# Value tiles ahead of the receptance tiles, and the recurrence queued one tile later with denser steps

## The chip, the cores and the metric

One Trainium2 chip, one of its cores. The metric is device time in microseconds (us) of the whole program, median of three runs. Next to it stands one profiled execution, whose trace supplies every duration quoted below. Engines: PE (TensorE), DVE (VectorE), ACT (ScalarE), POOL (GpSimd), SP (SyncE, here only an issuer of transfers). Each engine works through its instructions in the order in which the program emits them.

## The reference

Two layers, 1152 tokens (1024 of a prompt and 8 streams of 16 new tokens). In each layer one projection of the normalised input feeds four branches; their outputs are gated, projected back and added to the input.

```python
z = rms_norm(x, p['norm_g']) @ p['w_in']
za, zb = z[..., OFF_A:OFF_B], z[..., OFF_B:OFF_C]
zc, zd, gates = z[..., OFF_C:OFF_D], z[..., OFF_D:OFF_G], z[..., OFF_G:]
ya, shift_n, wkv_n = rwkv7_mix(za, shift0, s0, p)        # branch A
yd, pool_n = pool_mix(zd, None, p)                       # branch D
y = jnp.concatenate([ya, yb, yc, yd], axis=-1) * jax.nn.silu(gates)
out = x + y @ p['w_out']
```

The change concerns branch A, a delta-rule recurrence over tokens (per token `s = s*w + (s @ -kk) (kk*a) + v k`, `y = s r`), and branch D, trailing means over windows of 2, 4, 8 and 16 tokens minus the token itself, followed by a small linear map:

```python
ssum = c[:, j + 1] - c[:, lo, jnp.arange(POOL_GROUPS)[None, :]]
d = ssum / cnt[None, :, :, None] - xf[:, n_hist:]
out = jnp.einsum('btgc,gcd->btgd', d, p['pool_w'].astype(jnp.float32))
```

## The kernel before

The input projection of a layer is cut into 24 tiles of 128 output columns, in the order of `F_ORDER` (L35): the decay and rate inputs (WDAD), keys K0 and K1, receptance R0 and R1, values V0 and V1, pooling inputs D0 and D1 with their gates GD0 and GD1, then the other branches. `project` (L247) computes one tile for three groups of 384 tokens each; a group is 24 matmuls of 128 by 384 (high and low parts of the operands) into one of two PSUM buffers `pj`. After each group a sink function takes the buffer away: token shift for branch A (`shift_sink`, on ACT and DVE), trailing windows for D (`pool_in`: ACT copies at L802, POOL adds at L784, DVE subtracts at L791), gate and linear map for GD (`pool_gate`: ACT exponentials at L756 to L758, DVE L759, a PE matmul with `pbd`, DVE L820).

Between the matmuls stand ticks. A tick advances every lane by one step; lane "a" holds the generators of branch A in the order in which they were queued. `inproj` (L360) gives a tile its ticks: with `(2, 5)` a group has two inside and one behind it (three steps), with `(1, 3, 5)` four. Since the engines run in the order of emission, the place of a tick decides what stands ahead of what on PE, ACT, DVE and POOL.

Lane "a" holds, one behind the other: `a_elem` (elementwise work on a group, L428 to L487), `systems` (64 by 64 matmuls, scaled on DVE at L514 and written to a DRAM buffer by ACT's queue at L515), `solve` (L519: two triangular inverses, first on blocks of 16 and then of 32, all pairs of DVE operations at L538 and L540; then a copy at L550 and four transfers `dd` at L552 and L553, issued on ACT's queue), and `recurrence` (L707: 18 chunks of 64 tokens, the first two those of the streams, three steps a chunk). In a chunk ACT L610 and L636, DVE L655, L580 and L666, and PE's `b<-m,kbt` follow each other; L666 is the mask that the first two chunks need ahead of that matmul.

Of the kernel before, what the change touches and what calls it, by code (L numbers as in the profile page):

```python
# [31 lines left out]
(WDAD, K0, R0, V0, K1, R1, V1, D0, GD0, D1, GD1, VC0, VC1, U0, GC0, U1, GC1,  # L32
 GB0, GB1, Q0, Q1K, CK, GA0, GA1) = range(NF)

F_ORDER = (WDAD, K0, K1, R0, R1, V0, V1, D0, GD0, D1, GD1, VC0, VC1, U0, GC0, U1, GC1,  # L35
           Q0, Q1K, CK, GB0, GB1, GA0, GA1)


# [10 lines left out]
def tile_trunk(ctx: ExitStack, tc: tile.TileContext, *aps):  # L49
# [75 lines left out]
    def go(lane, gen):  # L125
        lanes.setdefault(lane, deque()).append(gen)

    def start(lane, gen):
        next(gen)
        go(lane, gen)  # L130
# [26 lines left out]
    def gcols(g):  # L157
        return slice(g * G, (g + 1) * G)
# [46 lines left out]
    SY.dma_start(out=vcs, in_=vec.rearrange("l p n -> p l n"))  # L205
    raw_weights(0, win[0, F_ORDER[0]])
    raw_weights(1, win[0, F_ORDER[1]])
    next(first[1])
# [136 lines left out]
    for l in range(L):  # L345
# [13 lines left out]

        def inproj(f, sink):  # L360
            ticks = (3,)
            if f in (K1, R0, R1, V0, V1, D0, GD0, D1, GD1, VC0, VC1, GC0, U1, GC1,
                     GA0, GA1):
                ticks = (2, 5)
            elif f in (U0, GB0, GB1):
                ticks = (1, 3, 5)
            project([(l, f)], xh, xl, [sink], ticks)

# [7 lines left out]
        def shift_sink(f, dest, after=None):  # L376
            last = {}

            def sink(g, ps):
                mu, om = vcol(V_MU + f), nv[:, f:f + 1]  # L380
                zs = dest(g)
                n = min(G, TP - g * G)
                A.activation(out=zs, in_=ps, func=AF.Copy, scale=om)
                if n == G:
                    last[g] = smp.tile([128, 1], F32, tag="lc", name=nm("lc"), bufs=4)
                    A.activation(out=last[g], in_=ps[:, G - 1:G], func=AF.Copy)
                V.scalar_tensor_tensor(out=zs[:, 1:n], in0=ps[:, 0:n - 1], scalar=mu, in1=zs[:, 1:n],
                                       op0=ALU.mult, op1=ALU.add)
                if g > 0:
                    V.scalar_tensor_tensor(out=zs[:, 0:1], in0=last[g - 1], scalar=mu, in1=zs[:, 0:1],  # L390
                                           op0=ALU.mult, op1=ALU.add)
                if n < G:
                    samp = ps[:, n:].rearrange("p (s t) -> p s t", t=SL)
                    zv = zs[:, n:].rearrange("p (s t) -> p s t", t=SL)
                    V.scalar_tensor_tensor(out=zv[:, :, 1:], in0=samp[:, :, :SL - 1], scalar=mu, in1=zv[:, :, 1:],
                                           op0=ALU.mult, op1=ALU.add)
                    V.scalar_tensor_tensor(out=zv[:, :, 0], in0=sh0[:, f, :], scalar=mu, in1=zv[:, :, 0],
                                           op0=ALU.mult, op1=ALU.add)
                    A.activation(out=sho[:, f, 0:1], in_=ps[:, n - 1:n], func=AF.Copy)
                    A.activation(out=sho[:, f, 1:], in_=samp[:, :, SL - 1], func=AF.Copy)  # L400
                if after:
                    after(g, zs)
            return sink

        def shifted(f, dest, after=None):
            inproj(f, shift_sink(f, dest, after))
# [20 lines left out]
        def a_elem(i, g, k):  # L427
            kb = abp.tile([128, 6, 2, 64], F32, tag="ab", name=nm("kb"))  # L428
            ar = abp.tile([128, 6, 2, 64], F32, tag="ab", name=nm("ar"))
            KB[i][g], AR[i][g] = kb, ar  # L430
            gc = gcols(g)

            def ea():
                return s_tile("ea", EA)

            q = ea()
            A.activation(out=q, in_=k, func=AF.Square, scale=vcol(V_KK + i))
            yield

            pw, pk, pa = st(), st(), pb()  # L440
            mm(pw[:, :G], wlo[0:64, i * 128:(i + 1) * 128], z6[0:64, gc])
            mm(pa[:, :G], wlo[64:128, i * 128:(i + 1) * 128], z6[64:128, gc])
            mm(pk[:, :G], bd1, q)
            rw, av = ea(), ea()
            A.activation(out=rw, in_=pw[:, :G], func=AF.Exp, scale=-1.0, bias=nv[:, 7 + i:8 + i])
            A.activation(out=av, in_=pa[:, :G], func=AF.Exp, scale=-1.0, bias=nv[:, 9 + i:10 + i])
            V.tensor_scalar(out=q, in0=pk[:, :G], scalar1=1e-24, scalar2=None, op0=ALU.max)
            recip1p(rw)
            cs = ea()
            n = min(G, TP - g * G)  # L450
            V.tensor_tensor_scan(out=cs, data0=smask[:, 0:G] if n == G else smask[:, 128:], data1=rw, initial=0.0,
                                 op0=ALU.mult, op1=ALU.add)
            yield
            A.activation(out=q, in_=q, func=AF.Ln)
            A.activation(out=q, in_=q, func=AF.Exp, scale=-0.5)
            ex = ar[:, :, 1, :]
            A.activation(out=ex, in_=chv(cs), func=AF.Exp, scale=-DECAY_C)
            nch = n // 64
            Po.tensor_copy(out=Pend[:, i, g * 6:g * 6 + nch], in_=ex[:, :nch, 63])
            if n < G:  # L460
                Po.tensor_copy(out=PendS[:, i, :].rearrange("p (c s) -> p c s", c=2),
                               in_=ex[:, nch:].rearrange("p c (s t) -> p c s t", t=SL)[:, :, :, SL - 1])
            V.tensor_tensor(out=rw, in0=cs, in1=rw, op=ALU.subtract)
            ep = rw
            A.activation(out=ep, in_=rw, func=AF.Exp, scale=-DECAY_C)
            ei = cs
            A.activation(out=ei, in_=cs, func=AF.Exp, scale=DECAY_C)
            yield

            kk = q  # L470
            V.scalar_tensor_tensor(out=kk, in0=k, scalar=vcol(V_KK + i), in1=q, op0=ALU.mult, op1=ALU.mult)
            V.scalar_tensor_tensor(out=ar[:, :, 0, :], in0=chv(kk), scalar=-1.0, in1=chv(ep),
                                   op0=ALU.mult, op1=ALU.mult)

            recip1p(av)
            yield
            t = ea()
            V.tensor_tensor(out=t, in0=av, in1=ei, op=ALU.mult)
            for hh in range(2):
                pr = slice(64 * hh, 64 * hh + 64)  # L480
                V.tensor_tensor(out=kb[pr, :, hh, :], in0=chv(kk)[pr], in1=chv(t)[pr], op=ALU.mult)  # L481
            V.tensor_scalar(out=av, in0=av, scalar1=vcol(V_KA + i), scalar2=nv[:, 11 + i:12 + i],
                            op0=ALU.mult, op1=ALU.add)
            V.tensor_tensor(out=av, in0=av, in1=ei, op=ALU.mult)
            for hh in range(2):
                pr = slice(64 * hh, 64 * hh + 64)
                V.tensor_tensor(out=kb[pr, :, 1 - hh, :], in0=chv(k)[pr], in1=chv(av)[pr], op=ALU.mult)  # L487

        def receptance(i, fr):
            def after(g, zs):  # L490
                ex = AR[i][g][:, :, 1, :]
                Po.tensor_tensor(out=ex, in0=chv(zs), in1=ex, op=ALU.mult)
            shifted(fr, lambda g: s_tile("gn", 3), after)

        def values(fv):
            v = m_tile()
            shifted(fv, lambda g: v[:, gcols(g)])
            vfm.append(v)
# [208 lines left out]
        def recurrence():  # L707

            seq = [16, 17] + list(range(16))
            yield from prepare(seq[0])  # L710
            for n, c in enumerate(seq):
                nxt = prepare(seq[n + 1]) if n < 17 else iter(())
                for _ in advance(c):
                    next(nxt, None)
                    yield
                for _ in nxt:
                    pass
                if c in (5, 11, 15):
                    go("n", groupnorm(c // 6))
                yield  # L720
# [184 lines left out]
        def after_k1(g, zs):  # L905
            start("a", a_elem(1, g, zs))
            if g > 0:
# [2 lines left out]
        project([(l, WDAD), (l, K0)], xh, xl,  # L910
                [shift_sink(WDAD, lambda g: z6[:, gcols(g)], tanh_part),
                 shift_sink(K0, lambda g: zk0[:, gcols(g)], lambda g, zs: start("a", a_elem(0, g, zs)))])
        shifted(K1, lambda g: zk1[:, gcols(g)], after_k1)
        go("a", idle(4))
        go("a", systems(2))
        go("a", idle(4))
        go("a", solve())
        receptance(0, R0)
        receptance(1, R1)
        values(V0)  # L920
        values(V1)
        A.dma_start(out=shift_o[l], in_=sho)
        pool_in(0, D0)
        go("a", recurrence())
        pool_gate(0, GD0)
        pool_in(1, D1)
        pool_gate(1, GD1)
        gating()
# [674 lines left out]
```

## Time and profile before

| | us |
|---|---|
| median of 3 runs | 1447.55 (1444.83 to 1448.42) |
| profiled execution | 1447.32 |
| span of the profiled execution | 1445.5 |
| PE busy | 1358.6 (94%) |
| DVE / ACT / POOL busy | 786.8 / 746.6 / 465.2 |

A timeline row gives start, duration, engine, line, operation and names, the count of merged instructions, and in brackets how long the engine had idled before and what released it. Matmul rows overlap: the distance between starts is what one costs. Times are of layer 1 (the second), in which K1 starts at 782, GD0 at 885 and D1 at 922; layer 0 runs the same tiles from 15 us on.

### The profile page before, as it was taken

Reading aid. Unit: us, or ns where it says so; the run is one execution under the profiler, and the core shown is the slowest. Engines: PE = TensorE matmul, PEld = TensorE weight load, DVE = VectorE, ACT = ScalarE, POOL = GpSimd, SP = SyncE. Lnnn points to the kernel's source line nnn. Section 1 sums busy time; section 2 is a strip of 40 time slices with the busy share of each in tenths; the row PEclk is TensorE's granted clock in tenths of the full one; section 3 lists DMA queues with packets and bytes.
Section 4 is the critical chain, followed back from the end, with each engine's and each line's share of the span. In section 5 each row is a group of like instructions: output and inputs, shape, how many; then the busy total and the mean of one; then the engine's idle time right before and its main releaser. Section 6 shows DMA issues by size and latency. Waiting matters only on the chain. (4 is left out here: it accounts for less than half of the span.)

```text
span 1445.5 us, 26910 instructions
## 1 busy us (share of the span) xinstructions
PE 1358.6 (94%) x9962; PEld 1160.2 (80%) x9962; DVE 786.8 (54%) x1766; ACT 746.6 (52%) x2013; POOL 465.2 (32%) x600
## 2 busy tenths in 40 slices
PE   4899989999999999999989998999999999899999
PEld 3768868888988886679977788788789788766998
DVE  6984954435235567742287948444532374777211
ACT  6762234655466677642257621555654676866210
POOL 4514404336411033332162234232653111322320
PEclk9799999999999999999999999999999999999999
DMA  7113241110312214033300122321022111131232
GB/s 222 52 32 75 63 102 42 61 49 25 96 46 70 60 37 128 5 116 93 99 22 30 49 64 66 92 69 49 29 71 74 52 57 59 45 103 45 74 95 77
DMA packets 116596, 97.40 MB, mean 67 GB/s; under 512 B 46129, under 2 KB 111345, under 8 KB 116465
## 3 DMA queue, kind: packets, MB, share of 16 engines
q1 hardware_dynamic: 76776, 73.74, 17.6%
q10 hardware_dynamic: 39688, 21.94, 5.1%
q8 instruction: 79, 1.29, 0.4%
q14 instruction: 53, 0.43, 0.1%
HBM read 71.48 MB, written 24.16 MB: 66 GB/s over the span
## 5 line engine op out<-in xcount | busy, mean ns | idle before, releaser
L76 PE MATMUL pj<-xh,wh 128*128 128x384 f32 x1152 | 415.4, 361 | 18.9 <-ACT xh L280 7.2
L76 PE MATMUL pj<-xl,wh 128*128 128x384 f32 x1152 | 396.4, 344 | 2.4 <-POOL xl L282 2.0
L76 PE MATMUL pj<-xh,wl 128*128 128x384 f32 x1152 | 396.3, 344 | 0.0
L242 POOL TENSOR_TENSOR wl<-wr,wh 128x256 fp32r<-128x256 f32 x200 | 157.0, 793 | 465.9 <-ACT wh L241 390.5
L76 PEld LDWEIGHTS pj<-xh,wh 128*128 128x128 f32 x1152 | 221.6, 193 | 41.7 <-ACT sho L400 11.3
L76 PEld LDWEIGHTS pj<-xl,wh 128*128 128x128 f32 x1152 | 222.1, 193 | 9.0 <-POOL xl L282 3.3
L76 PEld LDWEIGHTS pj<-xh,wl 128*128 128x128 f32 x1152 | 221.4, 192 | 6.0 <-issue 4.8
L76 PE MATMUL pj<-yh,wh 128*128 128x384 f32 x384 | 129.3, 337 | 2.4 <-DVE x L1426 2.4
L76 PE MATMUL pj<-yh,wl 128*128 128x384 f32 x384 | 128.6, 335 | 0.0
L76 PE MATMUL pj<-yl,wh 128*128 128x384 f32 x384 | 128.3, 334 | 0.0
L241 ACT ACTIVATE wh<-wr 128x256 fp32r<-128x256 f32 x200 | 81.0, 414 | 84.7 <-PE pj L76 41.0
L242 POOL TENSOR_TENSOR wl<-m,wh 128x256 fp32r<-128x256 f32 x56 | 43.7, 790 | 102.0 <-ACT wh L241 84.4
L76 PEld LDWEIGHTS pj<-yh,wh 128*128 128x128 f32 x384 | 72.1, 188 | 3.7 <-DVE x L1426 2.8
L76 PEld LDWEIGHTS pj<-yl,wh 128*128 128x128 f32 x384 | 72.1, 188 | 0.1
L76 PEld LDWEIGHTS pj<-yh,wl 128*128 128x128 f32 x384 | 72.1, 188 | 0.1
L1293 ACT ACTIVATE X<-b,ng 128x512 f32<-128x512 f32 (+3 forms) x96 | 55.0, 577 | 25.3 <-DVE ng L1285 21.4
L76 PE MATMUL b<-sp,cr 128*128 128x384 f32 (+3 forms) x192 | 59.5, 385 | 3.2 <-POOL sp L99 2.8
L1281 DVE TENSOR_REDUCE mx<-b 128x1 f32<-128x512 f32 (+3 forms) x96 | 53.0, 556 | 9.8 <-PE b L76 8.0
L1422 DVE TENSOR_TENSOR pt<-pj,pt 128x384 f32<-128x384 f32 x24 | 13.4, 557 | 80.6 <-PE pj L76 80.6
L76 PEld LDWEIGHTS st<-X,X 128*64 128x64 f32 x576 | 35.1, 136 | 27.4 <-ACT X L1311 7.6
L241 ACT ACTIVATE wh<-m 128x256 fp32r<-128x256 f32 x56 | 22.4, 413 | 61.0 <-PE pj L76 59.9
L1304 PE MATMUL pj<-cm,X 128*128 128x128 f32 x288 | 48.0, 286 | 5.0 <-ACT X L1293 5.0
(307 smaller groups left out, 2591.7 us busy)
## 6 DMA issues: line engine op xcount, KB each, us to landing
wr<-in_win_dram SPq DMA_DIRECT2D x176, 128.0 KB
m<-in_wout_dram SPq DMA_DIRECT2D x12, 512.0 KB
x<-in_xT_dram SPq DMA_DIRECT2D x12, 384.0 KB
ysp<-m ACTq DMA_DIRECT2D x24, 192.0 KB
pt<-in_xT_dram SPq DMA_DIRECT2D x24, 192.0 KB
ea<-ysp SPq DMA_DIRECT2D x24, 192.0 KB
x1d<-x ACTq DMA_DIRECT2D x24, 192.0 KB
pt<-x1d SPq DMA_DIRECT2D x24, 192.0 KB
```

The source lines that it names most:

```text
L76: return PE.matmul(out, lhsT=lhsT, rhs=rhs, start=start, stop=stop, skip_group_check=True)
L241: A.activation(out=h, in_=r, func=AF.Copy)
L242: Po.tensor_tensor(out=lo, in0=r, in1=h.bitcast(F32), op=ALU.subtract)
L1281: V.tensor_reduce(out=mx[:, b:b + 1], in_=pc[:, :w], axis=AX.X, op=ALU.max)
L1293: A.activation(out=P[:, :w], in_=pc[:, :w], func=AF.Exp, scale=SCALE, bias=ng, accum_out=sums[pr][:, b, s, h:h + 1])
L1304: PE.transpose(ptp[:, j * 128:(j + 1) * 128], Pb[slot][:, j * 128:(j + 1) * 128], ident)
L1422: V.tensor_tensor(out=xr, in0=ps, in1=xr, op=ALU.add)
```

## The change

Three edits. The tile order puts V0 behind K0, and V1 behind K1, ahead of R0 and R1; the calls that emit the tiles move with it. `recurrence` is queued behind GD0, not ahead of it, so that its first step falls into D1. D1 and GD1 get ticks `(1, 3, 5)`, four steps a group instead of three.

```diff
-F_ORDER = (WDAD, K0, K1, R0, R1, V0, V1, D0, GD0, D1, GD1, VC0, VC1, U0, GC0, U1, GC1,
+F_ORDER = (WDAD, K0, V0, K1, V1, R0, R1, D0, GD0, D1, GD1, VC0, VC1, U0, GC0, U1, GC1,
...
-            if f in (K1, R0, R1, V0, V1, D0, GD0, D1, GD1, VC0, VC1, GC0, U1, GC1,
+            if f in (K1, R0, R1, V0, V1, D0, GD0, VC0, VC1, GC0, U1, GC1,
...
-            elif f in (U0, GB0, GB1):
+            elif f in (D1, GD1, U0, GB0, GB1):
...
+        values(V0)
         shifted(K1, lambda g: zk1[:, gcols(g)], after_k1)
...
         go("a", solve())
+        values(V1)
         receptance(0, R0)
         receptance(1, R1)
-        values(V0)
-        values(V1)
...
+        pool_gate(0, GD0)
         go("a", recurrence())
-        pool_gate(0, GD0)
         pool_in(1, D1)
```

DVE in layer 1 where the inverse ends (L550) and the recurrence's first chunk goes on to its mask (L666), before:

```order
L550 COPY m_9334<-m_9335 128x1024
L655 TENSOR_TENSOR u_2042_9895<-b_9897,u_2042_9895 128x128
L580 TENSOR_TENSOR gm_9905<-b_9906,cm 128x256
L759 TENSOR_TENSOR pt_9881<-pj_9797,pt_9881 128x384
L580 TENSOR_TENSOR gm_9905<-b_9910,cm 128x256
L820 SCALAR_TENSOR_TENSOR m_9658<-st_9886,vcs,pt_9881 128x384
L759 TENSOR_TENSOR pt_9986<-pj_9924,pt_9986 128x384
L820 SCALAR_TENSOR_TENSOR m_9658<-st_9991,vcs,pt_9986 128x384
L666 TENSOR_SCALAR m_9941<-vu_9827,mseq_t 128x256 x4
```

and the same stretch now, in which `m_9924` is the result of D1's windows:

```order
L550 COPY m_9444<-m_9445 128x1024
L655 TENSOR_TENSOR u_2064_10011<-b_10013,u_2064_10011 128x128
L580 TENSOR_TENSOR gm_10021<-b_10022,cm 128x256
L791 SCALAR_TENSOR_TENSOR m_9924<-pt_10051,pinv_t,m_9923 64x384
L580 TENSOR_TENSOR gm_10021<-b_10026,cm 128x256
L791 SCALAR_TENSOR_TENSOR m_9924<-pt_10053,pinv_t,m_9923 64x384
L791 SCALAR_TENSOR_TENSOR m_9924<-pt_10175,pinv_t,m_9923 64x384
L791 SCALAR_TENSOR_TENSOR m_9924<-pt_10177,pinv_t,m_9923 64x384
L666 TENSOR_SCALAR m_10070<-vu_9955,mseq_t 128x256 x4
```

Between the copy and the mask two groups of GD0's gate (L759, L820) have given their place to two groups of D1's windows (L791).

ACT in the same place now, where the four `dd` transfers are issued, with the copies of D1's groups out of PSUM (L802) behind them:

```order
L552 DMA dd_291<-m_9445 64x32x32
L553 DMA dd_291<-m_9444 64x32x32
L552 DMA dd_291<-m_9445 64x32x32
L553 DMA dd_291<-m_9444 64x32x32
L610 ACTIVATE m_9997<-b_9964 128x2x128 x2
L636 ACTIVATE u_2064_10011<-b_10006 128x128
L802 ACTIVATE m_9923<-pj_9928 128x384
L802 ACTIVATE m_9923<-pj_10075 128x384
```

Before, L756 to L758 of GD0 stood where L802 stands now.

POOL now, the window sums that read those copies (`m_9923`) and that the L791 above wait for:

```order
L784 TENSOR_TENSOR pt_10047<-m_9923 128x398
L784 TENSOR_TENSOR pt_10049<-pt_10047 128x396
L784 TENSOR_TENSOR pt_10051<-pt_10049 128x392
L784 TENSOR_TENSOR pt_10053<-pt_10051 64x384
L796 TENSOR_TENSOR pf_10056<-pt_10051,pinv_t 64x16
L784 TENSOR_TENSOR pt_10171<-m_9923 128x398
L797 TENSOR_TENSOR m_9924<-pf_10056,m_9923 64x16
L796 TENSOR_TENSOR pf_10060<-pt_10053,pinv_t 64x16
L784 TENSOR_TENSOR pt_10173<-pt_10171 128x396
L784 TENSOR_TENSOR pt_10175<-pt_10173 128x392
L797 TENSOR_TENSOR m_9924<-pf_10060,m_9923 64x16
L784 TENSOR_TENSOR pt_10177<-pt_10175 64x384
```

Before, none of these stood between the copy L550 and the mask L666: D1 came a tile later.

## Rows read from the trace of the kernel before

**Rows 1.** The page: span, and shares of the chain that ended last, by engine.

```profile
span 1445.5 us, 26910 instructions
...
PE 33%; DVE 6%; ACT 2%; issue 1%; POOL 1%; DMA 1%; ACTq 0%; DVEq 0%; POOLq 0%
```

**Rows 2.** Busy time by stretch: PE, PEld, DVE, ACT, POOL, then clock, DMA, GB/s.

```profile
802.00:825.00 23.00, 21.07 (x160) 16.28 (x156) 20.49 (x41) 15.28 (x37) 6.57 (x10) 1.00 0.16 49
885.00:922.00 37.00, 31.46 (x312) 26.80 (x311) 25.21 (x57) 12.62 (x41) 9.07 (x13) 0.91 0.38 79
922.00:946.00 24.00, 24.00 (x296) 20.73 (x295) 9.83 (x21) 10.68 (x41) 12.28 (x17) 1.00 0.24 83
```

**Rows 3.** The same view, GD0 in layer 0.

```profile
173.00:210.00 37.00, 30.32 (x310) 25.77 (x310) 25.12 (x57) 12.62 (x41) 9.26 (x13) 0.95 0.40 79
```

**Rows 4.** Timeline of PE in GD0, layer 1.

```profile
892.88 0.81 PE L76 MATMUL st<-m,pbd 128*128 128x384 f32 x2
896.59 1.17 PE L76 MATMUL b<-vu,gm 64*64 64x64 f32 x8 [2.91 <-DVE gm L580]
908.38 0.34 PE L76 MATMUL pj<-xl,wh 128*128 128x384 f32 x1
910.64 0.34 PE L76 MATMUL pj<-xh,wl 128*128 128x384 f32 x1
912.23 1.08 PE L76 MATMUL b<-m,kbt 128*64 128x256 f32 x8 [1.25 <-DVE m L666]
```

**Rows 5.** Timeline of DVE, layer 1: the inverse and what follows it.

```profile
853.45 0.61 DVE L387 SCALAR_TENSOR_TENSOR m<-pj,vcs,m 128x383 f32<-128x383 f32 x1
855.34 0.52 DVE L538 TENSOR_TENSOR m<-m 32x15 f32<-32x15 f32 x1 [1.28 <-POOL wl L242]
864.00 0.19 DVE L538 TENSOR_TENSOR m<-m,m 128x31 f32<-128x31 f32 x1
...
898.75 1.08 DVE L550 COPY m<-m 128x1024 f32<-128x1024 f32 x1
907.49 0.56 DVE L759 TENSOR_TENSOR pt<-pj,pt 128x384 f32<-128x384 f32 x1 [0.55 <-ACT pt L758]
908.30 0.61 DVE L820 SCALAR_TENSOR_TENSOR m<-st,vcs,pt 128x384 f32<-128x384 f32 x1
909.94 2.15 DVE L666 TENSOR_SCALAR m<-vu,mseq_t 128x256 f32<-128x256 f32 x4
```

**Rows 6.** Timeline of ACT, layer 1: first and last `dd` issue, and what waits behind.

```profile
898.75 0.64 ACTq L552 DMA_DIRECT2D dd<-m  x1
...
903.33 1.50 ACTq L553 DMA_DIRECT2D dd<-m  x1
904.96 0.66 ACT L610 ACTIVATE m<-b 128x256 f32<-128x256 f32 x2 [13.51 <-PE pj L76]
905.88 0.30 ACT L636 ACTIVATE u<-b 128x128 f32<-128x128 f32 x1
```

**Rows 7.** Timeline of POOL, layer 1: the windows of D1's first group.

```profile
929.15 0.85 POOL L784 TENSOR_TENSOR pt<-m 128x398 f32<-128x398 f32 x1 [9.82 <-ACT m L802]
930.08 2.83 POOL L784 TENSOR_TENSOR pt<-pt 128x396 f32<-128x396 f32 x3
932.99 1.07 POOL L796 TENSOR_TENSOR pf<-pt,pinv_t 64x16 f32<-64x16 f32 x2
934.13 0.51 POOL L797 TENSOR_TENSOR m<-pf,m 64x16 f32<-64x16 f32 x2
```

**Rows 8.** Timeline of ACT, the copy of D1's first group.

```profile
928.52 0.49 ACT L802 ACTIVATE m<-pj 128x384 f32<-128x384 f32 x1 [0.64 <-PE pj L76]
```

**Rows 9.** Timeline of DVE: a window result of D0, and two of D1.

```profile
881.56 0.62 DVE L791 SCALAR_TENSOR_TENSOR m<-pt,pinv_t,m 64x384 f32<-64x384 f32 x1
...
931.87 2.11 DVE L791 SCALAR_TENSOR_TENSOR m<-pt,pinv_t,m 64x384 f32<-64x384 f32 x2 [1.58 <-POOL pt L784]
```

**Rows 10.** Waits of PE in U0, the tile with ticks (1, 3, 5).

```profile
PE b L76 <- DVE S L677: 1.2, 2, 0.9
```

## The prediction

> **What bounds the kernel now.** I read the page first: PE is the engine with the most to do and the one on which a third of the last chain lies [rows 1]. So I asked where PE stands still, stretch by stretch. In D1 it is busy all of 24.00 us at full clock; in GD0, of 37.00 us, only 31.46, and at a mean granted clock of 0.91 [rows 2]. Layer 0 shows the same tile with 30.32 us at 0.95 [rows 3]. GD0 is thus where a delay of branch A costs, and the stretch that the change works on.
>
> The timelines of GD0 say why. The inverse runs on DVE from 855.34 to the copy at 898.75 [rows 5]; the four transfers of its result are issued on ACT from 898.75 to 903.33 + 1.50 = 904.83, and ACT, which runs in order, can do nothing else: L610 comes at 904.96 after 13.51 idle [rows 6]. I call 904.83 T. From T the first chunk goes L610, L636, L655, L580, then the gate work of GD0 on DVE, then the mask L666 at 909.94 for 2.15, and PE's `b<-m,kbt` starts at 912.23, T + 7.4 [rows 4, 5, 6]. PE had run out of other work there, as it had at 896.59 for 2.91 [rows 4].
>
> **The change, part by part (layer 1; layer 0 is taken as equal).** What I follow is the start of that `b<-m,kbt`. It is a fair mark, since the work that PE has ahead of it differs by one known amount: one more tile. A bare group matmul costs (910.64 - 908.38) / 13 = 0.174 [rows 4], 72 of them 12.5; GD0's three `pbd` matmul pairs come ahead of the mark where two did, one pair 0.8 [rows 4]. So with PE losing as much as before the mark would lie at 912.2 + 13.3 = 925.5. A mark earlier than that is gain.
>
> *When T comes.* (a) The inverse starts where `systems` has delivered. The sinks ahead of it are three tiles, as before (V0, K1, part of V1 instead of K1, R0, part of R1), but K1, which feeds the second half of the elementwise work, now comes behind V0. DVE is busy 20.49 of 23 us there [rows 2], so V0's sinks are not free. A full group costs 0.61 [rows 5]; with the short one and the small pieces I estimate 2.7 a tile. Bounds: nothing, if the elementwise work on K0 fills the stretch anyhow, and 6, if both V tiles and a round of tick delays stand ahead. I take 2.0, start 857.3. (b) The inverse on blocks of 16 took 864.00 - 855.34 = 8.7, the short sink of V0 included [rows 5]; a full sink and two operations of R0's bonus (estimated from L820's 0.61) and their port conflicts join it: +2.6 (bounds 0.6 and 4). (c) The inverse on blocks of 32 took 34.7 [rows 5]. V1's sinks leave it (-2.7), all three gates of GD0 enter (3 x (0.56 + 0.61) = 3.5): +0.7 (bounds -1 and 3). (d) Copy and issue stay, 6.1. New T = 904.8 + 2.0 + 2.6 + 0.7 = 910.1. PE is covered until then by the extra tile, since T moves by 5.3 and the work by 13.3. Inside GD0 the gates behind invert steps on DVE hold `pj` buffers for some us; this costs nothing, as PE must wait for T in any case.
>
> *From T to the mark.* This is the step on which the forecast rests. Before, it took 7.4, with gate work of two groups in between. Now ACT has L610, L636 and then the copies L802 of D1's first two groups, which were computed while ACT was stuck in the issue; POOL's eight window sums wait for those copies; DVE's four L791 wait for the sums and stand ahead of the mask. So the wait for ACT's issue is followed by a whole pass through POOL. L610 0.13 + 0.66, L636 0.3, L802 0.3 of its 0.49 beyond the overlap [rows 6, 8] put POOL's start at T + 1.4. POOL: two groups of 0.85 + 2.83, 1.07 and 0.51 [rows 7], 8.9 in all, up to the last sum. One more L791 0.62 [rows 9], the mask 2.15 [rows 5], 0.1 to PE: T + 13.1, the mark at 923.2. Bounds: T + 11.5 if the small POOL operations fall away from the path and the mask takes 1.4; T + 15 if the L791 run at 1.05 each, as 2.11 for two beside POOL's windows shows [rows 9].
>
> The gap between 0.62 and 1.05 for the same L791 is one between an idle and a working POOL [rows 9]. The Trainium skill, "SBUF — State Buffer", section "SBUF: two separate sides", says that DVE with two SBUF inputs and a POOL operation that reads SBUF take a shared port pair as an exclusive lock, so the later of the two is fully blocked. By that, sums and L791 would not overlap at all and the mark would come about 1 us later than I put it; the 1.05 agrees in direction, and stands for the upper bound above without the rule.
>
> So at the mark 925.5 - 923.2 = 2.3 us are gained. *What comes after it.* PE has only 15 group matmuls (2.6 us) between T and the mark, so it idles some 7 us at one go. After the idling of GD0 the clock stood at 0.91 over 37 us, a loss of 3.3 [rows 2]; in layer 0 0.95, 1.9 [rows 3]. A part of it is in the 925.5 already; a new idle of 7 us should bring as much again: 2.0 (bounds 0 and 3.3). The state update of the next chunks stands on DVE behind L791 of D1's third group, for which DVE waits on POOL: 1.6, as DVE waits 1.58 ahead of L791 now, when nothing hangs on it [rows 9] (bounds 0 and 5.5, the windows of one group and more). Four steps a group instead of three leave six group matmuls between the steps of a chunk; U0, which has such ticks already, shows 1.2 us of PE waiting on the state [rows 10], and D1 and GD1 together I put at 1.2 (bounds 0 and 2.4). The tail is free: 54 steps fall into D1 to U0, where 57 fell into GD0 to U0; they end two steps into GC0, with DVE and ACT work there that PE does not wait for.
>
> Sum per layer: -2.3 + 2.0 + 1.6 + 1.2 = +2.5; two layers +5.0 on the profiled execution's 1447.32, which lies 0.2 under the median. Forecast 1452.3 us.
>
> **Rivals.**
> *A, the fast side.* The windows do not hold the mask, because D1's first groups are copied and summed before the issue takes ACT, so that only the third group comes behind it: the mark stays at T + 7.4, 917.5, and 8.0 us are gained. Minus 1.2 for density, 6.8 a layer: 1433.7. For it: DVE, POOL and ACT are far from busy in GD0 [rows 2] and only an order stands in the way. Against it: ACT cannot copy while it is stuck in the issue. The Trainium skill, "Perfetto Trace Analysis", section "Optimization Strategy", says that regimes with different busiest engines gain from interleaving; V tiles in the DVE-bound stretch are that. By it alone A would win; no row of before shows it.
> *B, a draw.* The mark as forecast, but idle clock and state update cost half, or were in the old GD0 too: -2.3 + 1.0 + 0.4 + 0.6 = -0.3 a layer, 1446.7; with neighbours 1443 to 1451. For it: old GD0 had its own half clock.
> *C, slower by more.* V0's and V1's sinks stand between the elementwise operations on DVE at its busiest [rows 2] and the inverse starts 6 later and not 2. T follows one for one, nothing covers it past the extra tile: +4.0 a layer more, 1460.3. It decides from a start of 861.
>
> **How the numbers follow.** Forecast 0.38 (its own range 1449 to 1457), A 0.22 (1429 to 1440), B 0.25 (1443 to 1451), C 0.15 (1456 to 1464). Less than 0.3% (4.3 us) either way cannot be told from no change in a measurement of this kernel. Faster: A and a quarter of B, 0.28. Same, 1443.2 to 1451.9: the rest of B and two fifths of the forecast, 0.34. Slower: the other three fifths and C, 0.38. The range that holds 8 in 10 goes from 1434 (leaving half of A) to 1460 (leaving half of C).
>
> **What would show it.** In the changed profile, layer 1: the first L538 at 857 (C: 861); T, the end of the last `dd` issue, at 910; L802 of D1's first two groups right behind T; eight L784 in a row on POOL and the four L791 ahead of L666; PE idle for about 7 us with DVE's L666 as releaser, and the mark at T + 13. A mark at T + 7 speaks for A. If PE does not idle there, or T is not on ACT's queue any more, the whole reading is wrong. A granted clock of 1.00 in D1 would take away the 2.0. If V0 and V1 shorten the stretch from K0 to R1 by several us, the gain is ahead of the mark, where I have put none.

## The result: 35 us slower, and where the profile after puts it

The changed kernel takes 1482.38 us (median of 4, 1477.67 to 1485.28) against 1447.72 in the same runs; the ratio is 1.024, interval 1.0207 to 1.0273. The forecast was 1452.3, its range ended at 1460. The profiled execution took 1477.67.

The page of the changed kernel, span and busy times:

```profile
span 1475.9 us, 26925 instructions
...
PE 1367.3 (93%) x9962; PEld 1169.2 (79%) x9962; DVE 791.1 (54%) x1766; ACT 744.6 (50%) x2013; POOL 465.3 (32%) x600
```

No engine has more instructions, and PE's 1358.6 have grown by 8.7 with the same matmuls, which run longer at half clock, the lower of the two levels of TensorE's granted clock (a stretch that holds both shows a mean such as 0.85). The span grew by 30.4 us, and the part of each layer from the tile behind K0 to the one ahead of Q0 holds nearly all of it. Its windows, the two of the kernel before and then the two of the changed kernel, layer 1 first in each pair (columns: PE, PEld, DVE, ACT, POOL busy, then clock, DMA share, GB/s):

```profile
782.00:1101.90 319.90, 302.90 (x2770) 263.85 (x2769) 177.24 (x405) 151.92 (x459) 123.40 (x161) 0.99 0.22 61
68.50:394.60 326.10, 305.34 (x2767) 265.72 (x2766) 177.33 (x407) 150.54 (x455) 123.48 (x161) 0.98 0.22 60
793.00:1131.30 338.30, 309.18 (x2769) 270.67 (x2768) 178.52 (x405) 151.07 (x459) 124.39 (x161) 0.96 0.22 57
66.90:404.10 337.20, 307.96 (x2768) 269.85 (x2767) 181.60 (x409) 150.89 (x459) 123.35 (x161) 0.96 0.22 58
```

So +18.4 and +11.1. In layer 1 PE idles 29.1 (width minus PE busy) against 17.0, and 0.04 x 338 = 13.5 went to the lower clock against some 3.

The same stretch of layer 1 in two parts, D0 to GD1 and then VC0 to U1, before (two lines) and after (two lines):

```profile
871.30:972.40 101.10, 94.37 (x985) 81.89 (x984) 58.08 (x126) 41.48 (x140) 37.38 (x53) 0.97 0.29 75
972.40:1086.40 114.00, 110.53 (x1153) 97.02 (x1153) 50.45 (x115) 63.45 (x200) 53.39 (x64) 1.00 0.18 53
878.90:993.10 114.20, 94.54 (x904) 82.36 (x904) 69.81 (x165) 38.03 (x126) 38.52 (x54) 0.91 0.30 68
993.10:1115.90 122.80, 116.67 (x1234) 102.09 (x1233) 52.66 (x121) 66.34 (x214) 56.53 (x66) 0.99 0.16 51
```

81 matmuls have moved from the first part to the second, since the recurrence starts a tile later, so the widths can't be compared directly, but the idle can. From D0 to GD1 it went from 6.7 to 19.7, and the clock from 0.97 to 0.91; from VC0 to U1 it went only from 3.5 to 6.1. In layer 0 the same parts went from 9.6 to 19.5 and from 5.0 to 6.4. Most of what the changed kernel lost against the one before it lost in D0 to GD1. The stretch from the tile behind K0 to the one ahead of D0, K1 to the V tiles, became shorter: 85.9 for 89.3 in layer 1, 85.3 for 90.8 in layer 0.

What PE waited for (line waited for, us in total, times, longest), two lines of the kernel before and then the changed kernel:

```profile
PE b L76 <- DVE m L666: 3.0, 4, 1.3
PE pj L76 <- DVE pt L759: 1.3, 2, 0.6
```

```profile
PE b L76 <- DVE m L666: 17.3, 4, 8.1
...
PE pj L76 <- DVE pt L759: 10.1, 2, 5.1
...
PE b L76 <- DVE gm L580: 5.6, 2, 2.8
...
PE b L76 <- ACT sp L96: 3.8, 2, 1.9
PE b L76 <- DMA tt<-dd: 3.6, 2, 1.9
```

The rise at L666 is twice 7 us. That at L759 is 8.8: the gates of GD0 now stand behind steps of the inverse on DVE, and PE waits for their `pj` buffers. The prediction put this at nothing, since PE must wait for T in any case; no run takes this wait alone out of the changed kernel.

Stage by stage in layer 1: GD0, D1, GD1, then U0 and GC0, to set beside [rows 2]:

```profile
896.30:918.50 22.20, 17.11 (x79) 16.09 (x78) 21.22 (x44) 5.59 (x13) 8.47 (x12) 0.85 0.36 78
918.50:953.40 34.90, 25.80 (x255) 22.06 (x254) 17.41 (x40) 8.75 (x30) 11.91 (x17) 0.85 0.31 60
953.40:993.10 39.70, 37.21 (x502) 30.09 (x501) 14.90 (x37) 20.33 (x76) 9.98 (x14) 1.00 0.31 80
1044.30:1081.10 36.80, 33.47 (x397) 28.26 (x395) 22.30 (x56) 22.78 (x83) 24.25 (x30) 0.95 0.09 28
1081.10:1103.40 22.30, 20.25 (x157) 17.59 (x154) 10.29 (x18) 11.45 (x28) 11.99 (x13) 1.00 0.14 45
```

GD0 became short, D1 long: 9.1 idle, and a clock of 0.85, that is 5.2 us, where before there was neither. GD0 itself loses 3.3 to the clock as it did before, U0 1.8 that it did not lose.

DVE of the changed kernel around the inverse and the mark, to set beside [rows 5] (layer 1 begins at 749.97 here and at 739.02 before, so 10.95 is taken off for any comparison):

```profile
876.58 0.16 DVE L538 TENSOR_TENSOR m<-m 32x15 f32<-32x15 f32 x1 [5.03 <-DMA m<-nds]
...
888.84 0.19 DVE L538 TENSOR_TENSOR m<-m,m 128x31 f32<-128x31 f32 x1
...
925.16 1.07 DVE L550 COPY m<-m 128x1024 f32<-128x1024 f32 x1
...
935.88 1.47 DVE L791 SCALAR_TENSOR_TENSOR m<-pt,pinv_t,m 64x384 f32<-64x384 f32 x1 [2.03 <-POOL pt L784]
...
942.47 1.18 DVE L791 SCALAR_TENSOR_TENSOR m<-pt,pinv_t,m 64x384 f32<-64x384 f32 x1 [0.89 <-POOL pt L784]
943.69 1.49 DVE L666 TENSOR_SCALAR m<-vu,mseq_t 128x256 f32<-128x256 f32 x4
```

ACT in the same place, to set beside [rows 6]:

```profile
929.32 2.50 ACTq L553 DMA_DIRECT2D dd<-m  x1
931.86 0.66 ACT L610 ACTIVATE m<-b 128x256 f32<-128x256 f32 x2 [7.64 <-PE pj L76]
932.41 0.28 ACT L636 ACTIVATE u<-b 128x128 f32<-128x128 f32 x1
932.57 0.89 ACT L802 ACTIVATE m<-pj 128x384 f32<-128x384 f32 x2
```

POOL, the first four and the last of the eight sums, to set beside [rows 7]:

```profile
933.15 0.85 POOL L784 TENSOR_TENSOR pt<-m 128x398 f32<-128x398 f32 x1 [13.36 <-DVE u L655]
934.08 2.86 POOL L784 TENSOR_TENSOR pt<-pt 128x396 f32<-128x396 f32 x3
...
941.13 1.31 POOL L784 TENSOR_TENSOR pt<-pt 64x384 f32<-64x384 f32 x1
```

PE at the mark, to set beside [rows 4]:

```profile
945.32 1.98 PE L76 MATMUL b<-m,kbt 128*64 128x256 f32 x8 [8.13 <-DVE m L666]
```

The reader is to see the chain of the forecast: T, the end of the last `dd` issue, is 929.32 + 2.50 = 931.82; the copies come right behind it, then the sums on POOL from 933.15 to 942.44, the last L791, the mask, and PE's matmul, the mark, after 8.13 idle at T + 13.5. On the layer's own time the inverse starts at 865.6, T is 920.9, the mark 934.4.

### The profile page after: what moved, and what is told of

It reads as the page before. It is cut to its first block, busy times and chain, and to the rows that moved or that the text cites. A ratio compares the mean times of both kernels' runs of the same rounds, so it can differ in the third digit from the quotient of the medians.

```text
span 1475.9 us, 26925 instructions
## 1 busy us (share of the span) xinstructions
PE 1367.3 (93%) x9962; PEld 1169.2 (79%) x9962; DVE 791.1 (54%) x1766; ACT 744.6 (50%) x2013; POOL 465.3 (32%) x600
## 4 chain that ended last, share of the span: by engine, by line
PE 65%; DVE 18%; DMA 5%; POOL 4%; ACT 4%; issue 3%; ACTq 1%; SPq 0%; DVEq 0%; POOLq 0%
PE pj L76 38%; PE b L76 14%; PE st L76 8%; PE pj L1304 3%; DMA nd<-ns 3%; DVE m L540 2%; DVE m L538 2%; DVE ea L278 2%; DMA tt<-dd 1%; POOL m L856 1%; POOL m L857 1%; DVE m L791 1%; POOL sp L99 1%; DVE ea L170 1%; PE b L586 1%
## 5 line engine op out<-in xcount | busy, mean ns | idle before, releaser
L76 PE MATMUL pj<-xh,wh 128*128 128x384 f32 x1152 | 418.0, 364 | 23.8 <-DVE pt L759 10.1
L76 PEld LDWEIGHTS pj<-xl,wh 128*128 128x128 f32 x1152 | 223.0, 194 | 13.1 <-POOL xl L282 4.9
L76 PE MATMUL st<-X,X 128*64 128x128 f32 x576 | 52.9, 285 | 0.0
```

Of the source, the lines that this page charges most:

```text
L76: return PE.matmul(out, lhsT=lhsT, rhs=rhs, start=start, stop=stop, skip_group_check=True)
```

## The experiments

All medians stand beside runs of the kernel before on the same chip (1446.3 to 1447.4 in the four groups of runs).

**Which part of the change costs.** Order alone: the tile order and the calls, nothing else.

```diff
-F_ORDER = (WDAD, K0, K1, R0, R1, V0, V1, D0, GD0, D1, GD1, VC0, VC1, U0, GC0, U1, GC1,
+F_ORDER = (WDAD, K0, V0, K1, V1, R0, R1, D0, GD0, D1, GD1, VC0, VC1, U0, GC0, U1, GC1,
...
+        values(V0)
...
+        values(V1)
...
-        values(V0)
-        values(V1)
```

> Only the tile order of the change (V0 behind K0, V1 behind K1, ahead of R0 and R1); the recurrence stays in GD0 and the ticks stay. Theory START (K1 comes a tile later, so that systems and the inverse start 10 us later in layer 1 and 5 to 6 in layer 0, as in the changed kernel, 865.5 against 855.3 from the layer's own start, and T, the end of the dd issue, follows): nothing covers it here, the mark stays at T + 7.4, +5 to +10 a layer, 1458 to 1468. Rival WINDOWS (the order is harmless or even good, the loss of the changed kernel lies between T and the mark and in the clock): 1440 to 1449.

Measured 1463.86, ratio 1.0106 (1.0067 to 1.0144). The inverse started at 127.1 from the start of layer 1 (before 116.3) and 135.2 in layer 0 (127.7). That fits START. But the mark did not stay at T + 7.4: it came 4 us ahead of T. The mark needs no `dd`; where it waits for T it waits in ACT's queue alone. D1 took 45.4 us for 23.8:

```profile
917.20:962.60 45.40, 37.75 (x414) 30.80 (x413) 20.45 (x46) 15.66 (x60) 13.69 (x20) 0.85 0.35 86
```

PE idles 7.7 there and the clock fell to 0.85; most of the rest is work that GD0, at 26.0 for 36.8, no longer holds.

The late recurrence alone:

```diff
-        go("a", recurrence())
         pool_gate(0, GD0)
+        go("a", recurrence())
```

> Only the recurrence queued behind GD0; old tile order, ticks (2, 5) in D1 and GD1. Theory START: T stays near 905, the mark is at T + 13, 918, against a parity of 925.5; 7 us gained a layer at the mark, about 5 given back by the half clock after PE's idle and by the waits behind it: 1440 to 1450. Rival WINDOWS: the pass through POOL and what follows it is the loss by itself, +8 to +15 a layer as in the changed kernel, 1463 to 1477.

Measured 1447.18, ratio 1.000 (0.9982 to 1.0018): harmless. The mark lies at T + 19.6 here, not T + 13, yet PE idles only 1.22 for it. Its rows on ACT, the end of the issue and D1's first copy:

```profile
902.26 1.51 ACTq L553 DMA_DIRECT2D dd<-m  x1
...
916.67 0.49 ACT L802 ACTIVATE m<-pj 128x384 f32<-128x384 f32 x1 [3.01 <-DMA ysp<-m]
```

and on POOL, the sums of that group:

```profile
917.24 0.85 POOL L784 TENSOR_TENSOR pt<-m 128x398 f32<-128x398 f32 x1 [4.35 <-ACT m L802]
918.17 2.85 POOL L784 TENSOR_TENSOR pt<-pt 128x396 f32<-128x396 f32 x3
```

T is 903.8, 13 us ahead of the copy. D1 starts behind T, so its groups are copied as they come and only one group's sums stand ahead of the mask, beside matmuls.

The dense steps on top of the late recurrence, in the old order (the edit against the late recurrence alone):

```diff
-            if f in (K1, R0, R1, V0, V1, D0, GD0, D1, GD1, VC0, VC1, GC0, U1, GC1,
+            if f in (K1, R0, R1, V0, V1, D0, GD0, VC0, VC1, GC0, U1, GC1,
...
-            elif f in (U0, GB0, GB1):
+            elif f in (D1, GD1, U0, GB0, GB1):
```

> Recurrence behind GD0 and ticks (1, 3, 5) in D1 and GD1; old tile order. Theory START: as with the late recurrence alone, and a recurrence that ends 7 steps earlier: within 3 of that run, 1438 to 1450. Rival DENSE (four steps a group cost PE by themselves, in the changed kernel 9.9 us a layer are lost behind the mark): 8 to 15 above the run with the late recurrence alone.

Measured 1471.32, ratio 1.0161 (1.012 to 1.0201): 24 above the late recurrence alone. In the old order the dense steps, which the forecast put at 1.2 a layer, are the largest of the three parts. The other order with K1 left in place:

```diff
-F_ORDER = (WDAD, K0, K1, R0, R1, V0, V1, D0, GD0, D1, GD1, VC0, VC1, U0, GC0, U1, GC1,
+F_ORDER = (WDAD, K0, K1, V0, V1, R0, R1, D0, GD0, D1, GD1, VC0, VC1, U0, GC0, U1, GC1,
...
-        receptance(0, R0)
-        receptance(1, R1)
...
+        receptance(0, R0)
+        receptance(1, R1)
```

> Order WDAD, K0, K1, V0, V1, R0, R1; recurrence and ticks as before. K1 is where it was, so that the elementwise work and systems start as before. Theory START: T within 2 of 904.8, 1444 to 1451. Rival (V tiles ahead of R are costly wherever they stand, since their sinks sit between the elementwise operations): T 4 or more later in each layer, 1455 or more.

Measured 1453.69, ratio 1.005 (1.0028 to 1.0072), between the two. The inverse starts as before (115.5 in layer 1), but its second part takes 38 instead of 35 us, and T comes 4.2 later there, 1.5 in layer 0. Of the 17 us of the order alone, 10 thus go with K1's place, and some 7 stay with V tiles ahead of R.

**Within the changed kernel.** Ticks (2, 5) again in D1 and GD1:

> The changed kernel with ticks (2, 5) in D1 and GD1 again: the tile order and the late recurrence alone. Theory THREE TERMS (the order costs 17 alone, the late recurrence nothing, the dense steps 24, each by its own mechanism; the order is partly covered by the late recurrence): 1455 to 1464. Rival WINDOWS (the pass through POOL ahead of the mask is the main loss, and it is still there): 1472 or more.

Measured 1466.33, ratio 1.0139 (1.0104 to 1.0174), just outside the expected stretch: sparse steps do not bring back what the order lost, and the mark still is at T + 13.3 with 8.12 idle. The dense steps cost 16 in the changed kernel, against 24 in the old order. Then U0 sparse instead, in the old order with the dense steps:

> Late recurrence and dense D1 and GD1 in the old tile order, with U0 at ticks (2, 5), so that U0 takes three steps a group and not four and the recurrence ends later in GC0. Theory TAIL (the dense steps lose their time in U0 and GC0, where the end of the recurrence meets the groupnorm and the SGU work: 2.7 and 1.9 of idle and the half clock after it, some 8 a layer): 1455 to 1462 against 1471. Rival (dense steps lose it where they are, in D1 and GD1): 1468 to 1475.

Measured 1470.93, ratio 1.0173 (1.0142 to 1.0204): the rival's number, by another road. U0 lost its idle (0.1 for 3.2), but GC0 got 6.7. The loss moved to wherever the recurrence ended.

D1's sums left out of the changed kernel, so that the second half of branch D is not computed (`i` is 1 for D1):

```diff
-                while w < w0[1]:
+                while w < w0[1] and not i:
...
-                    sw = got[w0[half]]
...
+                    sw = z if i else got[w0[half]]
...
-                    if first:
+                    if first and not i:
```

> The changed kernel without the window sums of D1: POOL's L784, L796 and L797 are left out there and L791 reads the copied group itself, so branch D's second half is not the reference's. Theory WINDOWS AT THE MARK (the 13.5 us from T to the mark are the pass through POOL): T + 6 to T + 8, 6 us a layer at the mark and the half clock behind it, 12 to 18 below the changed kernel, 1464 to 1470. Rival (PE waits there for something else that comes as late): within 4 of the changed kernel.

Measured 1464.48, ratio 1.0128 (1.0094 to 1.0161): 18 below the changed kernel, as expected. PE's row at the mark, T + 6.6:

```profile
931.78 1.08 PE L76 MATMUL b<-m,kbt 128*64 128x256 f32 x8 [1.75 <-DVE m L666]
```

The idle fell from 8.13 to 1.75, and D1 ran at full clock. WINDOWS AT THE MARK holds. What the kernel before would gain by the same omission was not measured, so a part of the 18 may be the work itself and not its place.

D1 ahead of GD0, in the old order of K, R and V, with the recurrence queued behind D1:

```diff
-F_ORDER = (WDAD, K0, K1, R0, R1, V0, V1, D0, GD0, D1, GD1, VC0, VC1, U0, GC0, U1, GC1,
+F_ORDER = (WDAD, K0, K1, R0, R1, V0, V1, D0, D1, GD0, GD1, VC0, VC1, U0, GC0, U1, GC1,
...
+        pool_in(1, D1)
...
-        pool_in(1, D1)
```

> Old order of K, R and V, but D1 ahead of GD0 (D0, D1, GD0, GD1), recurrence behind D1, ticks as before. D1's copies and sums then lie beside the inverse and ahead of T, and the gates of GD0 behind T as before. Theory QUEUE ORDER (what stands on ACT and DVE beside the inverse decides): the 5 us that PE waits for GD0's gates in the run with the late recurrence go away, the mark stays near T + 7 with a tile more ahead of it: 1432 to 1444. Rival (the recurrence's later end gives everything back in GC0 and U1, as in that run): 1445 to 1452.

Measured 1449.76, ratio 1.0023 (1.0008 to 1.0039): no gain. The waits for GD0's gates went and those for L666 fell to 1.1, but PE waited for the load of the start state instead, 10.8 in all against 4.1 in the run with the late recurrence. The rival's number, for a reason that neither had named.

**The tail.** The old order with late recurrence and dense D1 and GD1, now with fewer steps in VC0 and VC1, so that the end meets the same tiles as with the late recurrence alone (the edit against the run with the dense steps):

```diff
-            if f in (K1, R0, R1, V0, V1, D0, GD0, VC0, VC1, GC0, U1, GC1,
+            if f in (K1, R0, R1, V0, V1, D0, GD0, GC0, U1, GC1,
```

> Late recurrence and dense D1 and GD1 (1, 3, 5) in the old tile order, and VC0 and VC1 with ticks (3,), two steps a group, so that U0, GC0 and U1 meet the same chunks of the recurrence as in the run with the late recurrence alone. Theory TAIL (two thirds of what the dense steps cost, 24 us, is lost where the recurrence ends between U0 and GC0): 1446 to 1455. Rival IN PLACE (dense steps cost where they stand, in D1 and GD1): 1463 to 1474.

Measured 1452.78, ratio 1.0049 (1.0032 to 1.0066). 18.5 of the 24 went away with the place of the end; 5.6 stay. TAIL holds. U0 in layer 1, with the dense steps and then with this edit:

```profile
1036.20:1076.00 39.80, 36.57 (x398) 30.57 (x396) 22.69 (x56) 22.78 (x83) 23.92 (x30) 0.87 0.08 26
1017.10:1048.40 31.30, 31.30 (x404) 26.58 (x401) 17.71 (x51) 19.55 (x77) 19.41 (x26) 1.00 0.14 43
```

The fewer steps in VC0 and VC1 are not what was gained there: with the dense steps these tiles hold only 0.0 and 0.8 of idle in layer 1. Why the place matters, DVE in U0 of the changed kernel:

```profile
1064.98 0.61 DVE L728 SCALAR_TENSOR_TENSOR gn<-ar,vcs,kb 64x384 f32<-64x384 f32 x1 [3.70 <-POOL gn L748]
1065.52 0.53 DVE L855 TENSOR_SCALAR m<-st,mv,rs 128x256 f32<-128x256 f32 x1
1065.97 0.74 DVE L580 TENSOR_TENSOR gm<-b,cm 128x256 f32<-128x256 f32 x2
```

The groupnorm's first DVE operation waits 3.70 for POOL, where operations of the gating unit (L856, L857) stand ahead of L748 from 1056.93 to 1064.00; behind it stands L580 of the recurrence, and PE idles 2.81 for that. The steps at the end of the recurrence are not only the chunk's own: the groupnorm and the gating unit stand between them in the queues.

**The issue on ACT.** The four transfers on SP's queue, in the kernel before:

```diff
-                A.dma_start(out=diagonal(dd, i, 32, 128), in_=DT[64 * i:64 * i + 64])
-                A.dma_start(out=diagonal(dd, i, 32, 128, 64), in_=DN[64 * i:64 * i + 64])
+                SY.dma_start(out=diagonal(dd, i, 32, 128), in_=DT[64 * i:64 * i + 64])
+                SY.dma_start(out=diagonal(dd, i, 32, 128, 64), in_=DN[64 * i:64 * i + 64])
```

> The kernel before with the four dd transfers (L552, L553) issued on SP's queue and not on ACT's; SP has nothing to do there from 896 to 908. Theory QUEUE (the first chunk needs no dd, it waits only because ACT is taken by the issue until T): L610 comes right behind the copy, at 900 and not at 905, the mark 4 to 6 earlier, and as PE waits there for little more than 2 us a layer, 3 to 6 us in all: 1441 to 1445. Rival (the chunk waits for the end of the inverse on DVE in any case, or SP is late with weights): 1446 to 1451.

Measured 1449.86, ratio 1.0025 (1.0011 to 1.0038): a miss. The mark came earlier by 7 to 8 and its idle went, but the next consumer, which does need the data, took over:

```profile
918.23 0.42 PE L76 MATMUL b<-tt,gm 64*64 64x32 f32 x8 [3.68 <-DMA tt<-dd]
```

The same in the run with the late recurrence:

> Late recurrence, and the dd issue on SP. PE waits for L666 by 3.7 a layer, for the start state by 2 and for GD0's gates by 5 in the run with the late recurrence alone. Theory QUEUE: the waits for L666 go: 1439 to 1445. Rival: no change against that run, 1446 to 1449.

Measured 1442.68, ratio 0.9978 (0.9967 to 0.999): the time was in the expected stretch, though not for the expected reason, since PE's waits for L666 stayed at 7.4 in all; what went were the waits for the start state, 4.1, and some half-clock time (mean clock 0.989 against 0.983 in the profiled executions). The same in the changed kernel:

> The changed kernel with the dd issue on SP. Theory QUEUE (the two copies L802 are held by the issue, and so the windows come behind T): the mark comes 6 earlier and the idle ahead of it, 8.1, falls to 2 to 4; with the half clock behind it 10 to 18 below the changed kernel, 1464 to 1472. Rival (the windows hold the mask wherever the issue is): within 5 of the changed kernel, 1477 to 1485.

Measured 1472.68, ratio 1.0182 (1.0164 to 1.0201): 10 below, just above the expected stretch. The mark came 4.5 earlier, and the idle at it fell to 4.52, a little above what QUEUE said. So somewhat under half of the wait, 3.6 of 8.13, was the stuck copies.

**Do the terms add up?** K1 first again, with the late recurrence and ticks (2, 5):

> Order K0, K1, V0, V1, R0, R1, late recurrence, ticks (2, 5): the run of order and late recurrence (1466) with K1 ahead of V0 again. Theory START (the order costs because K1's elementwise work and systems begin 8 us later): the inverse starts at 116 from the layer's start and not at 126, 1447 to 1455. Rival (V tiles ahead of R cost as such): 1460 or more.

Measured 1454.74, ratio 1.0051 (1.0034 to 1.0068), 11.6 below its partner, the changed kernel with ticks (2, 5). The start of the inverse in the partner, where layer 1 begins at 748.58, and here, where it begins at 743.33:

```profile
874.94 0.16 DVE L538 TENSOR_TENSOR m<-m 32x15 f32<-32x15 f32 x1 [4.93 <-DMA m<-nds]
859.61 0.72 DVE L538 TENSOR_TENSOR m<-m 32x15 f32<-32x15 f32 x1 [1.75 <-POOL ar L492]
```

That is 126.4 and 116.3 into the layer. T is 170.1 and no longer 182.0, D1's groups come behind T, and the mark idles 1.2 for 8.1. START holds for these 11.6, and it is the late T that brings the windows in front of the mask. Some 7 above the late recurrence alone remain, the V tiles ahead of R, as in the run with K1 in place.

The tail out of the changed kernel:

> The changed kernel with VC0 and VC1 at ticks (3,), so that U0 to U1 meet the end of the recurrence as in the run with the late recurrence alone. Theory TAIL adds up: 16 to 20 below the changed kernel, 1461 to 1467. Rival (the tail's cost comes from the delay that the windows make, both cannot be taken away twice): 1472 or more.

Measured 1460.69, ratio 1.0092 (1.0078 to 1.0105): 21.7 below, a little more than expected. Its U0 and GC0, to set beside the last two stage rows above:

```profile
1025.60:1056.90 31.30, 31.30 (x404) 26.59 (x401) 17.68 (x51) 19.53 (x77) 19.37 (x26) 1.00 0.14 43
1056.90:1082.20 25.30, 25.30 (x291) 21.52 (x290) 12.36 (x27) 15.78 (x47) 10.51 (x12) 1.00 0.14 46
```

No idle and full clock in both tiles. The 21.7 are not all loss against the kernel before, whose U0 idles 3.05 in layer 1 itself: this edit also takes away what was lost there from the start. Tail and windows out together:

> The changed kernel without D1's window sums (L784, L796, L797 left out there, L791 on the copied group) and with VC0 and VC1 at ticks (3,). THREE TERMS: windows 18 and tail 18 away from 1482 leave the order and the start, 1445 to 1452. Rival (the order costs its 17 by itself on top): 1456 or more.

Measured 1445.49, ratio 0.9993 (0.9983 to 1.0002): level with the kernel before. That is a balance. D0 to GD1 and VC0 to U1 of layer 1, to set beside the two pairs in the section on the result:

```profile
866.00:968.40 102.40, 90.06 (x906) 78.55 (x905) 65.78 (x161) 38.14 (x126) 22.16 (x32) 0.97 0.30 74
968.40:1083.60 115.20, 114.25 (x1233) 100.26 (x1231) 52.54 (x121) 67.62 (x214) 54.18 (x63) 1.00 0.17 53
```

From D0 to GD1 PE still idles 12.3, against 6.7 before (13.8 against 9.6 in layer 0); from VC0 to U1 it idles less than before, 0.95 for 3.5 (1.1 for 5.0). The order's later T is still there (182.3 in layer 1). It is not free; what it costs is made up by a tail that is better than the old one, and by the shorter stretch of the K, R and V tiles (88.6 for 89.3 in layer 1, 85.7 for 90.8 in layer 0).

The last one looks for a kernel that beats both:

> D1 ahead of GD0, recurrence behind D1, and the dd issue on SP. With the issue on ACT PE idled 5.3 in D1, since the copies L802 stood behind the issue. Theory QUEUE: that idle and its half clock go: 1437 to 1443, below the 1442.7 of the late recurrence with the issue on SP or equal to it. Rival (the wait moves to the load of dd, as when the issue alone was moved): 1445 to 1450.

Measured 1443.68, ratio 0.9974 (0.9961 to 0.9986), just above the expected stretch. It and the late recurrence with the issue on SP both beat the kernel before by about a quarter of a per cent; their intervals overlap. Here too PE waits for the load of the start state (L566), 13.2 in all, so the expected reason, ACT's stuck copies, was not what bound that order.

## Why the prediction was wrong, step by step

*T to the mark: right.* T + 13.1 forecast, T + 13.5 measured; PE's idle "some 7" against 8.13 with L666 as releaser. The stuck copies and the four L791 ahead of the mask are there as written, and leaving the sums out shows the mechanism (T + 6.6). The sum came out so near partly because its errors cancel: POOL's pass took 9.3 for 8.9 and the last L791 1.18 for 0.62, but the mask 1.49 for 2.15.

*The start of the inverse: wrong, and the first step that failed.* "I take 2.0, start 857.3", bounds 0 and 6. Measured 865.6, 10.3 later; in layer 0 6.0. The working counted sinks on DVE and supposed that K0's elementwise work would fill the stretch. What set the start is when K1's groups exist: the second half of the elementwise work and `systems` hang on K1, and K1 starts 18 us later in layer 1 (61.1 for 43.0) and is 5 shorter. It is one tile of PE, not 2.7 us of DVE. Putting K1 ahead of V0 again brought the start back to 116.3 and 11.6 us with it. Of the 11.2 by which the mark missed its forecast (934.4 for 923.2), 8.3 are this; the inverse's two parts were 0.9 and 1.0 longer than forecast, the issue 0.5, the rest 0.4. In the working of the inverse's second part -2.7 and 3.5 make 0.8, not 0.7, which changes nothing. Rival C named a late start and its sign, a start from 861 on, and put the time at 1460.3 with a chance of 0.15. Its mechanism was another, V's sinks between the elementwise operations on DVE. The run with V tiles ahead of R and K1 in place speaks against that: the inverse starts there at 115.5, as before.

*The gain at the mark: sign wrong by that.* T was to come 5.3 later, and PE to be covered by the extra tile; T came 16.1 later in layer 1 and 11.2 in layer 0. 2.3 us were to be gained a layer; 925.5 - 934.4 = -8.9 came in layer 1, and -4.0 in layer 0.

*The clock: mis-sized.* 2.0 was taken and 3.3 bounded. Layer 1 lost about 10 more than before: D1 5.2, U0 1.8, and smaller stretches at 0.95 and less elsewhere. In that layer idles of 5.1 (GD0), 8.13 (D1) and 2.81 (U0) were followed by time at half clock, while GC0 with an idle of 1.90 ran at 1.00; there were more such idles than the one counted.

*"The tail is free": wrong.* It was argued from where the recurrence ends, with "DVE and ACT work there that PE does not wait for". PE waits for it (2.81 and 1.90 behind L580 and L96 in layer 1), since in the queues it stands ahead of the recurrence. Moving the end without touching D1 and GD1 brought 21.7 back. Set beside the kernel before, whose own tail was not free either, VC0 to U1 idles 2.7 more in layer 1 and 1.4 in layer 0, so this is the smaller part of the loss. The 1.2 for density itself was too low as well: the 5.6 for two layers that stay in the old order, 2.8 a layer, lie above its bound of 2.4, and no run separates them from the fewer steps in VC0 and VC1.

*The state update: no wait of that size.* The 1.6 a layer behind the mark did not show: in the changed kernel PE waits for the state only 0.3 there in layer 1.

*The gain from interleaving.* The prediction's last line names a gain ahead of the mark where it had put none. The stretch from the tile behind K0 to D0 did become shorter by 3.4 in layer 1 and 5.5 in layer 0. That regimes with different busiest engines gain from interleaving, as the prediction has it beside rival A, is a possibility and no promise: the order alone cost 17.

*The sum.* Taken out of the changed kernel, windows bring 18, tail 22, together 37. This is not how the loss of 35 against the kernel before is made up: there the idle from D0 to GD1 grew by 12.9 in layer 1 and 10.0 in layer 0, with the clock from 0.97 to 0.91 and from 0.98 to 0.92, and that from VC0 to U1 by 2.7 and 1.4. The forecast failed first at one late start that turned a gain into a wait with the windows behind it, and then at a changed end of the recurrence that was taken as nothing.

## What to carry to other kernels

When a tile is moved, follow what hangs on the tiles that it displaces: here K1's place was 10 of the 17 us that the order cost alone, and the V tiles ahead of R the other 7. When steps are made denser, look where their chain ends and whose work stands in the queues there; an earlier end is not better by itself. An experiment that takes a queue wait away shows what the next wait is, and that one may be on data. When two edits to the changed kernel bring its time back to the old one, compare the stages with the kernel before: the same time can be another balance.

## What was not expected of the hardware

Three long idles of PE in layer 1 of the changed kernel were followed by stretches at the lower of the two levels of the granted clock: in D1 9.1 us of idle came with 5.2 us lost to the clock, and behind the mark the eight matmuls that take 1.08 us in [rows 4] took 1.98. There the idle has to be priced with that: in that layer 13.5 us on 29.1 of idle, where before it was some 3 on 17.0.

In four cases of these two traces a slow L791 beside a working POOL reads as a wait for POOL's operation. The one at 935.88 takes 1.47 and ends 0.41 behind POOL's sums (934.08 + 2.86 = 936.94); two others of the changed kernel end 0.41 to 0.42 behind the POOL operation beside them, and so does the first of the two in [rows 9], which takes 1.46 while the second takes 0.62. POOL waits too: its last sum took 1.31, starting while an L791 ran until 941.58, and ended 0.86 after it. So the traces agree with the full block in the prediction's sentence on the port; the 1.05 that it read there is the mean of two unlike ones.
